# S5 states worked in place in PSUM: VectorE's products with one operand in a PSUM bank, and GpSimd's part between states and outputs dropped

## The chip, the cores and the metric

One core of a Trainium2 chip runs the kernel. The metric is the device time of the execution in microseconds, the median of several runs. PE is the matrix engine, DVE (VectorE), ACT (ScalarE) and POOL (GpSimd) work on SBUF; DVE and ACT also reach the PSUM banks into which PE writes, POOL does not in this kernel. SP issues DMA transfers. Each engine works through its own queue in order; semaphores hold an instruction until what it needs is done, and everything behind it on that engine waits too.

## The reference

A two-layer streaming encoder, one step: 512 tokens of a new stream and 32 of a running one, width 1024. Layer 0 mixes tokens with an S5 state-space layer and a GLU, layer 1 with retention; each layer then has attention to 256 memory tokens and a causal ConvFFN. The part that matters here:

```python
def s5_block(state, u, a_bar, b_bar, c):
    bu = jnp.einsum('gpc,blgc->blgp', b_bar, u.astype(jnp.complex64))
    bu = bu.at[:, 0].add(a_bar * state)
    a = jnp.broadcast_to(a_bar, bu.shape)
    _, xs = lax.associative_scan(_linear_combine, (a, bu), axis=1)
    y = jnp.real(jnp.einsum('gcp,blgp->blgc', c, xs))
    return xs[:, -1], y
...
    y = from_chunks(y).reshape(bsz, l, D_MODEL) + d.astype(F32) * hf
    g = jax.nn.gelu(y)
    out = g * jax.nn.sigmoid(g @ w_glu.astype(F32) + b_glu.astype(F32))
```

There are 64 groups of 16 channels, each with 64 complex states; `hf` is the RMS norm of x. The memory projections of both layers (`memory_kv`, 256 x 1024 by 1024 x 2048 each) depend on no token and can run at any time.

## The kernel before

Everything up to the GLU is `phase1`. Time is cut into blocks of 8 steps: 64 block positions for the prompt, 4 for the sample, and a few for initial states make POS = 70 positions. The recursion over 70 positions is a real scan, once the complex phase of each state is taken out: states are multiplied by a table of phases `pr`, `pi` (32 states a partition x 70), scanned with the real decay, and multiplied back. The channels are done in eight parts, e = 0 to 7 ("eighths": 8 groups each), and each eighth has six steps, which are functions inside `phase1`:

- **V** `powers(e)`: scales u by the RMS factor `ur` (POOL, L821) and forms powers of A times B: four VectorE products of 512 elements a partition (L829, L830) and two POOL additions (L831).
- **M** `matrices(e)`: PE transposes the powers (L843), ACT copies them out (L844); PE and ACT form the block's own matrix (L848, L850, L851), VectorE adds (Fg, L855) and SP spreads Fg by eight transfers (M<-Fg, L858).
- **S** `states(e)`: PE forms block inputs in two PSUM banks (L869, tile "bank"); VectorE multiplies by the phases (L884, L885, L887, L888: 280 elements), POOL subtracts and adds (L886, L889), and copies the initial state in (L890, L891).
- **Z** `scan(e)`: two VectorE scans (L902); four products by the phases, two on VectorE (L904, L906) and two on POOL (L905, L907); four sums L911/L912 of 64 partitions, which give S; ACT copies the end states into `stout` (L914, L915).
- **C** `carry(e)`: six VectorE instructions of 512 elements (L928, L930, L932) that form Y from the output coefficients `ca`.
- **O** `outputs(e)`: PE adds u by M (L943) and S by Y (L944) in a bank, ACT applies gelu (L945), PE transposes (L953), ACT copies out (L955, L956). The GLU's matmuls (L249) need all eight.

Between these steps `fill` puts pieces of the memory projections, which keep PE busy: layer 0 in plain fp32 (L528), layer 1 in two-part fp32 with three matmuls (L240, L241, L242). For layer 1 each weight tile is loaded (wr, L226), rounded on ACT (wh, L229), negated on ACT (wl, L230) and completed by an adding transfer that POOL issues (L235). Their results leave PSUM by VectorE (L550) or ACT (L565); L491 and L492 scale the memory tokens.

`PROLOGUE` and `ORDER` give the order in which the program writes these steps (at step e: S, C of e+1, V of e+3, Z of e+1, O of e, projections, M of e+2, projections). It is not the order of the queues: the framework plays the program through a timeline of its own (`schedule_with_timeline_sim=True`) and sorts each engine's instructions by it. The phase table is built by doubling in `phases` (L585 and L588 on POOL, L584, L586, L587, L589 on VectorE; L770 to L779 are the short chain that squares the phase). `ur` comes from a sum of squares on PE (L744), its reduction L746, and a short VectorE chain to L331. PSUM has eight banks in one ring (`bank()`), used in turn; SBUF has 28 slots "r" (`slot()`) and 8 slots "xl".

## Time and profile before

| what | us |
|---|---|
| median of 3 runs | 1877.81 (1876.53 to 1879.45) |
| the profiled execution | 1877.61 |
| its span | 1875.8 |
| PE busy in the span | 1814.0 |
| DVE busy | 1062.9 |
| ACT busy | 628.9 |
| POOL busy | 342.7 |
| first GLU matmul (L249) starts at | 233.61 |

Times in the profile are from the span's start. A group's row has its line, engine, operation, tiles (out<-in), shapes and count, then busy time and the mean of one in ns, then idle time of the engine ahead of it and what ended it. In the rows of the chain of waits and of the timeline the first number is the start, the second the length; the chain counts a piece up to where the next one begins, so that an instruction is shorter there by the overlap with its follower.

### The profile page before, as it was taken

To read this page: it belongs to the slowest core of one execution; us is meant where nothing else is said; L and a number is where in the kernel's file an instruction comes from. 1 tells how busy PE (TensorE), PEld (TensorE's weight loads), DVE (VectorE), ACT (ScalarE), POOL (GpSimd) and SP (SyncE) were. 2 spreads that over 40 slices of the span, in tenths; PEclk is the share of its full clock that TensorE was granted. 3 is DMA by queue.
4 is the path that set the end of the run, shared out by engine and by line. 5 is a ranking of instruction groups with operands and counts; after the bars stand their busy time and mean duration, and the time that the engine had idled before them with its cause. 6 is when DMAs were issued, how large, how long until landed. Compare 5 with 4: busy or idle time off the path is not lost.

```text
span 1875.8 us, 32777 instructions
## 1 busy us (share of the span) xinstructions
PE 1814.0 (97%) x13815; PEld 1727.9 (92%) x13815; DVE 1062.9 (57%) x1795; ACT 628.9 (34%) x933; POOL 342.7 (18%) x416
## 2 busy tenths in 40 slices
PE   8778899999999999999999999999999999999998
PEld 7467699999999999999899899998899999999997
DVE  8988875455535545555545645547654554453553
ACT  3244554343313323333123222223443332232333
POOL 4655410021202202220000100100101121120221
PEclk9978999999999999999999999999999999999999
DMA  6647743132222222222222222222312222222221
GB/s 227 201 122 176 193 159 103 56 107 82 90 83 86 82 99 89 82 91 85 82 88 85 71 88 74 91 79 90 124 68 68 79 91 90 84 81 96 90 72 68
DMA packets 68274, 186.41 MB, mean 99 GB/s; under 512 B 9184, under 2 KB 18784, under 8 KB 68128
## 3 DMA queue, kind: packets, MB, share of 16 engines
q1 hardware_dynamic: 65536, 175.79, 28.3%
q0 software_dynamic: 2304, 8.39, 2.5%
q8 instruction: 108, 1.77, 0.4%
q14 instruction: 38, 0.31, 0.1%
q10 hardware_dynamic: 288, 0.15, 0.0%
HBM read 171.16 MB, written 10.77 MB: 97 GB/s over the span
## 4 chain that ended last, share of the span: by engine, by line
PE 85%; DVE 8%; DMA 2%; issue 2%; ACT 2%; POOL 1%; SPq 0%; DVEq 0%; ACTq 0%; POOLq 0%
PE ps L249 75%; PE ps L240 2%; PE ps L241 2%; PE ps L242 2%; DMA M<-Fg 1%; DMA wr<-in_w_v 1%; PE ps L1341 1%; DVE r L902 1%; POOL u L821 1%; DVE r L830 1%; DVE wl L209 0%; PE ps L1330 0%; DVE r L930 0%; ACT wh L208 0%; PE ps L1303 0%
## 5 line engine op out<-in xcount | busy, mean ns | idle before, releaser
L249 PE MATMUL ps<-xh,wh 128*128 128x272 f32 x2432 | 505.2, 289 | 5.5 <-DVE x L372 3.7
L249 PE MATMUL ps<-xh,wl 128*128 128x272 f32 x2432 | 503.6, 288 | 0.0
L249 PE MATMUL ps<-xl,wh 128*128 128x272 f32 x2432 | 502.4, 288 | 0.0
L208 ACT CAST wh<-wr 128x1024 fp32r<-128x1024 f32 (+1 forms) x240 | 248.1, 1038 | 757.4 <-PE ps L249 640.0
L249 PE MATMUL ps<-r,wh 128*128 128x272 f32 x2688 | 448.1, 288 | 2.9 <-ACT r L956 1.6
L249 PEld LDWEIGHTS ps<-xh,wh 128*128 128x128 f32 x2432 | 381.8, 188 | 11.2 <-ACT r L314 3.8
L249 PEld LDWEIGHTS ps<-r,wh 128*128 128x128 f32 x2688 | 379.4, 188 | 6.3 <-ACT r L208 3.0
L249 PEld LDWEIGHTS ps<-xh,wl 128*128 128x128 f32 x2432 | 381.2, 188 | 2.3 <-issue 2.3
L249 PEld LDWEIGHTS ps<-xl,wh 128*128 128x128 f32 x2432 | 381.9, 188 | 0.3
L209 DVE TENSOR_TENSOR wl<-wr,wh 128x1024 fp32r<-128x1024 f32 (+1 forms) x240 | 296.1, 1237 | 94.9 <-ACT wh L208 86.7
L249 PE MATMUL ps<-r,wl 128*128 128x272 f32 x1344 | 277.9, 288 | 0.0
L249 PEld LDWEIGHTS ps<-r,wl 128*128 128x128 f32 x1344 | 210.7, 188 | 0.0
L372 DVE TENSOR_TENSOR x<-ps,x 128x544 f32<-128x544 f32 x96 | 69.3, 724 | 235.3 <-PE ps L249 234.9
L317 POOL TENSOR_TENSOR acc<-acc,r 128x544 f32<-128x544 f32 x36 | 59.2, 1645 | 452.4 <-ACT r L314 443.9
L1150 DVE TENSOR_TENSOR r<-ps,rr 128x544 f32<-128x544 f32 x44 | 31.9, 724 | 95.5 <-PE ps L249 95.5
L1140 DVE TENSOR_TENSOR r<-ps,rr 128x272 f32<-128x272 f32 x44 | 19.4, 442 | 116.9 <-PE ps L249 116.9
L1143 POOL COPY nco<-r 128x2 f32<-128x2 f32 x44 | 13.1, 297 | 373.5 <-DVE r L1141 373.5
L208 ACT CAST r<-r 128x544 fp32r<-128x544 f32 x84 | 52.5, 650 | 65.5 <-POOL r L1151 25.9
L1201 POOL TENSOR_TENSOR r<-r,r 128x544 f32<-128x544 f32 x8 | 10.8, 1354 | 339.7 <-ACT wh L208 325.7
L1151 POOL TENSOR_TENSOR r<-r,r 128x32 f32<-128x32 f32 x44 | 35.0, 795 | 206.3 <-ACT wh L208 191.1
L1148 DVE SCALAR_TENSOR_TENSOR r<-r,conv,r 128x546 f32<-128x546 f32 x88 | 69.1, 785 | 3.5 <-ACT r L1146 2.0
L209 DVE TENSOR_TENSOR r<-r,r 128x544 fp32r<-128x544 f32 x84 | 59.3, 728 | 10.6 <-ACT r L208 10.4
(347 smaller groups left out, 2102.0 us busy)
## 6 DMA issues: line engine op xcount, KB each, us to landing
wr<-in_w_r SPq DMA_DIRECT2D x48, 512.0 KB, 3.3
wr<-in_w_a SPq DMA_DIRECT2D x44, 512.0 KB, 3.2
wr<-in_w_g SPq DMA_DIRECT2D x44, 512.0 KB, 3.3
wr<-in_w_d SPq DMA_DIRECT2D x32, 448.0 KB, 3.3
wr<-in_w_k SPq DMA_DIRECT2D x16, 512.0 KB, 4.1
wr<-in_w_v SPq DMA_DIRECT2D x16, 512.0 KB, 4.0
wr<-in_w_q SPq DMA_DIRECT2D x16, 512.0 KB, 3.8
wr<-in_w_o SPq DMA_DIRECT2D x16, 512.0 KB, 3.3
```

The lines of the kernel that those rows point to most:

```text
L208: self.nc.scalar.copy(hi, src)
L209: (self.nc.gpsimd if pool else self.nc.vector).tensor_tensor(out=lo, in0=src, in1=hi.bitcast(F32), op=OP.subtract)
L240: mm(out, lhsT=a[0], rhs=b[0], start=start, stop=False)
L241: mm(out, lhsT=a[0], rhs=b[1], start=False, stop=False)
L242: mm(out, lhsT=a[1], rhs=b[0], start=False, stop=stop)
L249: mm(ps[:, h, :TH], lhsT=ws[wi], rhs=x[xi][:, h * TH:(h + 1) * TH], start=start and n == 0, stop=stop and n == 2)
L317: add.tensor_tensor(out=self.acc, in0=self.acc, in1=sq, op=OP.add)
L372: self.nc.vector.tensor_tensor(out=self.halves(x), in0=src, in1=self.halves(x), op=OP.add)
L1140: V.tensor_tensor(out=ext[:, 2:2 + TH], in0=pa[:, 0, :TH], in1=r[:, :TH], op=OP.mult)
L1148: V.scalar_tensor_tensor(out=cv, in0=ext[:, t:t + W], scalar=cw[:, t, f:f + 1], in1=cv, op0=OP.mult, op1=OP.add)
L1150: V.tensor_tensor(out=self.halves(gr), in0=pg[:, :, :TH], in1=self.halves(r), op=OP.mult)
L1151: PL.tensor_tensor(out=gr[:, TP:], in0=gr[:, TP:], in1=cv[:, TP + 2:W], op=OP.mult)
```

## The change

The state banks stay in use from PE's products until the sums: S multiplies into SBUF and in place in the bank, the subtraction and the addition are VectorE's and write the bank, the scan works in place on the bank, and so does one of each pair of products behind it. So each VectorE instruction there has one operand in PSUM and at most one in SBUF. POOL's L886, L889, L905 and L907 go to VectorE; its copies L890 and L891 go to ACT (L899, L898). The coefficients that C and V read are copied by ACT into free columns of the state banks (columns 280 to 408: `ca`, L880; 408 to 472: the b coefficients of eighth e+2, L884, for e = 1 to 5; those of eighths 0 to 2 lie in a bank of their own, L816). C's second product goes into a bank of the ring instead of an SBUF slot, and the load of `ca` is issued in S instead of C. New line numbers: L821 is L826, L829/L830/L831 are L834/L835/L836, L844 is L849, L855 is L860, L869 is L876, the products of S are L893/L894, the subtraction and addition L897/L896, the scan L915, its products L916/L917, the sums L921/L922, `stout` L924/L925, C is L938/L940/L942, gelu L955, the outputs' matmuls L953/L954.

```diff
+        b3 = self.bank()[:, :384].rearrange("p (n e i c) -> p n e i c", n=2, e=3, i=4)
+        for n in range(2):
+            A.copy(b3[:, n], bb[n][:, :12].rearrange("p (e i) c -> p e i c", e=3))
+        bbe = {e: [b3[:, n, e] for n in range(2)] for e in range(3)}
...
-            bs = [a[:, p0:p0 + 4].unsqueeze(2).to_broadcast(sh) for a in bb]
+            bs = [a.unsqueeze(2).to_broadcast(sh) for a in bbe.pop(e, [b[:, p0:p0 + 4] for b in bb])]
...
         def states(e):
+            ca = load("ca", [P, 2, 8, C], io["ca"][e].rearrange("p (r n c) -> p r n c", r=2, n=8), 2)
+            banks = [self.bank() for _ in range(2)]
+            d["v"] = v = [b[:, :280].rearrange("p (n q) -> p n q", n=4) for b in banks]
...
+            d["ca"] = [b[:, 280:408].rearrange("p (n c) -> p n c", c=C) for b in banks]
+            for n in range(2):
+                A.copy(d["ca"][n], ca[:, n])
+            if e and e + 2 < KT:
+                bbe[e + 2] = [b[:, 408:472].rearrange("p (n c) -> p n c", c=C) for b in banks]
+                for n in range(2):
+                    A.copy(bbe[e + 2][n], bb[n][:, p0 + 8:p0 + 12])
...
-            V.tensor_tensor(out=w[0], in0=vps[0], in1=phs[0], op=OP.mult)
-            V.tensor_tensor(out=x1[0], in0=vps[1], in1=phs[1], op=OP.mult)
-            PL.tensor_tensor(out=w[0], in0=w[0], in1=x1[0], op=OP.subtract)
-            V.tensor_tensor(out=w[1], in0=vps[1], in1=phs[0], op=OP.mult)
-            V.tensor_tensor(out=x1[1], in0=vps[0], in1=phs[1], op=OP.mult)
-            PL.tensor_tensor(out=w[1], in0=w[1], in1=x1[1], op=OP.add)
-            PL.tensor_copy(out=w[0][:, :, 65], in_=s0[:, p0:p0 + 4])
-            PL.tensor_copy(out=w[1][:, :, 65], in_=s0n[:, p0:p0 + 4])
+            x = d["x"] = pair()
+            for n in range(2):
+                V.tensor_tensor(out=x[n], in0=v[n], in1=phs[0], op=OP.mult)
+                V.tensor_tensor(out=v[n], in0=v[n], in1=phs[1], op=OP.mult)
+            V.tensor_tensor(out=v[1], in0=x[0], in1=v[1], op=OP.subtract)
+            V.tensor_tensor(out=v[0], in0=x[1], in1=v[0], op=OP.add)
+            A.copy(v[1][:, :, 65], s0[:, p0:p0 + 4])
+            A.copy(v[0][:, :, 65], s0n[:, p0:p0 + 4])
...
         def scan(e):
+            z = d["v"][::-1]
+            x = pair()
             for n in range(2):
-                V.tensor_tensor_scan(out=z[n].rearrange("p n q -> p (n q)"), data0=d0.rearrange("p n q -> p (n q)"),
-                                     data1=w[n].rearrange("p n q -> p (n q)"), initial=0.0, op0=OP.mult, op1=OP.add)
-            V.tensor_tensor(out=x1[0], in0=z[0], in1=phs[0], op=OP.mult)
-            PL.tensor_tensor(out=x1[1], in0=z[1], in1=phs[1], op=OP.mult)
-            V.tensor_tensor(out=x2[0], in0=z[1], in1=phs[0], op=OP.mult)
-            PL.tensor_tensor(out=x2[1], in0=z[0], in1=phs[1], op=OP.mult)
+                zn = z[n].rearrange("p n q -> p (n q)")
+                V.tensor_tensor_scan(out=zn, data0=d0, data1=zn, initial=0.0, op0=OP.mult, op1=OP.add)
+                V.tensor_tensor(out=x[n], in0=z[n], in1=phs[0], op=OP.mult)
+                V.tensor_tensor(out=z[n], in0=z[n], in1=phs[1], op=OP.mult)
...
         def carry(e):
-            ca = load("ca", [P, 2, 8, C], io["ca"][e].rearrange("p (r n c) -> p r n c", r=2, n=8), 2)
+            ca = d["ca"]
...
-                y, yt = xl(512), self.slot(512)
+                y, yt = xl(512), self.bank()
```

The change also alters the sorted order of the queues. Three places follow, each with the queue before and then after; r is an SBUF slot, bank a PSUM bank, and a number behind a name tells one tile from another.

POOL before, from the phase table's products (ph) to the scaling of u:

```order
L585 TENSOR_TENSOR r_608<-ph_506 128x480
L588 TENSOR_TENSOR r_609<-ph_506 128x480
L585 TENSOR_TENSOR r_616<-ph_506 128x512
L588 TENSOR_TENSOR r_617<-ph_506 128x512
L831 TENSOR_TENSOR r_673<-r_673,r_675 128x512
L831 TENSOR_TENSOR r_674<-r_674,r_676 128x512
L821 TENSOR_TENSOR u_158<-u_158,ur_451 128x560
L821 TENSOR_TENSOR u_159<-u_159,ur_451 128x560
```

POOL now, in the same part of the program:

```order
L826 TENSOR_TENSOR u_164<-u_164,ur_451 128x560
L826 TENSOR_TENSOR u_165<-u_165,ur_451 128x560
L585 TENSOR_TENSOR r_551<-ph_506 128x32
L588 TENSOR_TENSOR r_552<-ph_506 128x32
L836 TENSOR_TENSOR r_516<-r_516,r_518 128x512
L836 TENSOR_TENSOR r_517<-r_517,r_519 128x512
L807 COPY ph_506<-ph_506 128x32x5
L585 TENSOR_TENSOR r_566<-ph_506 128x96
L588 TENSOR_TENSOR r_567<-ph_506 128x96
```

The eight scalings of u stood behind all products of the phase table; now all of these, from the first doubling (128x32) on, stand behind the scalings.

VectorE before, from the first carry to the scan of eighth 0:

```order
L928 TENSOR_TENSOR xl_717<-ca_715,Pr_351 128x512
L928 TENSOR_TENSOR xl_722<-ca_715,Pr_351 128x512
L884 TENSOR_TENSOR r_703<-bank_683,ph_506 128x280
L888 TENSOR_TENSOR r_704<-bank_683,ph_506 128x280
L855 TENSOR_TENSOR Fg_659<-bank_647,Fg_659 128x128
L885 TENSOR_TENSOR r_704<-bank_692,ph_506 128x280
L887 TENSOR_TENSOR r_703<-bank_692,ph_506 128x280
L930 TENSOR_TENSOR r_718<-ca_715,ait_381 128x512
L930 TENSOR_TENSOR r_723<-ca_715,ait_381 128x512
L928 TENSOR_TENSOR xl_874<-ca_872,Pr_351 128x512
L928 TENSOR_TENSOR xl_879<-ca_872,Pr_351 128x512
L932 TENSOR_TENSOR xl_717<-xl_717,r_718 128x512
```

VectorE now, from the first products of eighth 0 on:

```order
L893 TENSOR_TENSOR r_710<-bank_688,ph_506 128x280
L893 TENSOR_TENSOR r_710<-bank_689,ph_506 128x280
L894 TENSOR_TENSOR bank_688<-bank_688,ph_506 128x280
L894 TENSOR_TENSOR bank_689<-bank_689,ph_506 128x280
L897 TENSOR_TENSOR bank_688<-r_710,bank_688 128x280
L896 TENSOR_TENSOR bank_689<-r_710,bank_689 128x280
L938 TENSOR_TENSOR xl_719<-bank_688,Pr_351 128x512
L938 TENSOR_TENSOR xl_724<-bank_688,Pr_351 128x512
L940 TENSOR_TENSOR bank_720<-bank_689,ait_381 128x512
L940 TENSOR_TENSOR bank_725<-bank_689,ait_381 128x512
L915 SCALAR_TENSOR_TENSOR bank_688<-d_150_708,bank_688 128x280
L942 TENSOR_TENSOR xl_719<-xl_719,bank_720 128x512
```

The carry of eighth 0 stood ahead of its products and partly beside POOL's work; now its products come first, the subtraction and addition follow on VectorE, and the carry behind them reads and writes banks.

ACT before, from the copy of eighth 2's end states on (wh and wl are rounded weights of the projections):

```order
L914 COPY stout_498<-r_1100 128x8
L915 COPY stout_498<-r_1100 128x8
L229 CAST wh_1218<-wr_1216 128x1024
L844 COPY xl_1178<-bank_1180 128x512
L844 COPY xl_1179<-bank_1186 128x512
L230 ACTIVATE wl_1219<-wh_1218 128x1024
L850 COPY ft_1201<-bank_1192 128x128
L229 CAST wh_1253<-wr_1251 128x1024
L230 ACTIVATE wl_1254<-wh_1253 128x1024
L229 CAST wh_1394<-wr_1392 128x1024
L230 ACTIVATE wl_1395<-wh_1394 128x1024
```

ACT now, from the end states of eighth 2 on, with the copies into the banks of eighth 3 (bank_1294, bank_1295):

```order
L924 COPY stout_498<-r_1107 128x8
L925 COPY stout_498<-r_1107 128x8
L849 COPY xl_1185<-bank_1187 128x512
L849 COPY xl_1186<-bank_1193 128x512
L230 ACTIVATE wl_1226<-wh_1225 128x1024
L855 COPY ft_1208<-bank_1199 128x128
L229 CAST wh_1260<-wr_1258 128x1024
L230 ACTIVATE wl_1261<-wh_1260 128x1024
L229 CAST wh_1403<-wr_1401 128x1024
L880 COPY bank_1294<-ca_1292 128x128
L230 ACTIVATE wl_1404<-wh_1403 128x1024
L884 COPY bank_1294<-bbr_402 128x64
```

The copies of the coefficients stand behind the copy of the end states and behind the conversions of the projections' weights, mixed with them.

More of the change, by code (lines that the diff above doesn't have):

```diff
@@ L881, in states, with pair @@
                              in1=rho8[:, p0:p0 + 4].unsqueeze(2).to_broadcast(pos3), op=OP.mult)
[L882 to L892 removed]
+            x = d["x"] = pair()
[6 more added lines that the diff above has]
+            A.copy(v[0][:, :, 65], s0n[:, p0:p0 + 4])
+        def pair():
+            t = self.slot(SLOT)
+            return [t[:, n * 280:(n + 1) * 280].rearrange("p (n q) -> p n q", n=4) for n in range(2)]
         def scan(e):
@@ L910, in scan @@
                 r = slice(64 * g2, 64 * g2 + 64)
[L911 to L912 removed]
+                V.tensor_tensor(out=SS[0:64, :, g2], in0=x[0][r], in1=z[1][r], op=OP.add)
+                V.tensor_tensor(out=SS[64:128, :, g2], in0=x[1][r], in1=z[0][r], op=OP.subtract)
             S = d["S"] = SS.rearrange("p n g q -> p (n g) q")
```

21 lines of the change are left out of this document (4 added, 17 removed).

## The prediction

> **What bounds the kernel now.** I read the windows first, to find the stage that the change touches and who is busy in it, then PE's waits there, then VectorE's groups by shape, and at last the chain of waits through the stage. The windows' columns: from:to, length, then busy time (and instructions) of PE, PEld, DVE, ACT and POOL, the granted clock, the DMA share, GB/s.
>
> ```profile
> 93.00:234.00 141.00, 111.17 (x951) 97.41 (x952) 119.54 (x178) 64.85 (x128) 71.14 (x78) 0.88 0.66 164
> 180.00:220.00 40.00, 36.54 (x328) 30.71 (x328) 33.84 (x51) 20.44 (x36) 20.66 (x26) 0.99 0.88 211
> 234.00:1875.80 1641.80, 1623.78 (x12485) 1574.75 (x12483) 863.11 (x1404) 537.22 (x762) 219.44 (x276) 1.00 0.26 87
> ```
>
> Behind 234 us PE works 1623.78 of 1641.80 us at full clock. The built order of PE is the same there before and after: its last 12,271 matmuls stand in the same sequence. So the whole change is what it does to the time at which the GLU's first matmul (L249) starts; that shift passes through one to one. Ahead of it, from 93 to 234, PE idles 141.00 - 111.17 = 29.8 us and VectorE is busy 119.5 of 141.
>
> ```profile
> PE bank L944 <- DVE r L911: 8.5, 2, 7.8
> PE bank L944 <- DVE r L912: 6.3, 1, 6.3
> PE bank L241 <- DVE r L492: 5.2, 1, 5.2
> ```
>
> PE's longest waits in this stage are for VectorE: for an eighth's sums L911/L912 (the outputs' second matmul needs them), and for L492. The groups of VectorE, and the same lines in the chain of waits (start, length; the lengths run from start to start):
>
> ```profile
> L930 DVE TENSOR_TENSOR r<-ca,ait 128x512 f32<-128x512 f32 x16 | 20.1, 1294 | 0.0
> L932 DVE TENSOR_TENSOR xl<-xl,r 128x512 f32<-128x512 f32 x16 | 16.4, 1058 | 0.0
> L928 DVE TENSOR_TENSOR xl<-ca,Pr 128x512 f32<-128x512 f32 x15 | 14.0, 971 | 0.1
> L902 DVE TENSOR_TENSOR_SCAN r<-d,r 128x280 f32<-128x280 f32 x16 | 13.7, 890 | 1.9 <-POOL r L890 1.8
> L884 DVE TENSOR_TENSOR r<-bank,ph 128x280 f32<-128x280 f32 x8 | 3.6, 445 | 0.6 <-PE bank L869 0.5
> L855 DVE TENSOR_TENSOR Fg<-bank,Fg 128x128 f32<-128x128 f32 x8 | 2.3, 282 | 2.0 <-PE bank L851 2.0
> ```
>
> ```profile
> 92.97 0.45 DVE r L911
> ...
> 110.43 1.58 DVE r L492 x4
> ...
> 118.70 0.35 DVE r L887
> ...
> 120.86 1.29 DVE r L930 x2
> 122.15 0.60 DVE r L829
> ...
> 171.13 1.28 DVE r L902 x2
> ...
> 220.58 1.20 DVE xl L932 x2
> ...
> 226.43 0.46 DVE r L911
> ...
> 233.61 2.40 PE ps L249 x17
> ```
>
> With POOL out of the way a 512-wide product or sum takes 0.60 us and a scan 0.64; the means of the same lines are 0.97 to 1.29 and 0.89. The products that read PSUM (L884) stay at 0.445 busy, 0.35 from start to start. From the last sum of eighth 0 (92.97+0.45 = 93.42) to that of eighth 7 (226.89) the recursion takes 133.5 us; the GLU follows 6.7 us later, at 233.61.
>
> **What leaves and what is added.** POOL loses six instructions an eighth:
>
> ```profile
> L889 POOL TENSOR_TENSOR r<-r,r 128x280 f32<-128x280 f32 x8 | 8.8, 1100 | 0.0
> L907 POOL TENSOR_TENSOR r<-r,ph 128x280 f32<-128x280 f32 x8 | 8.6, 1081 | 6.8 <-DVE r L902 6.8
> L905 POOL TENSOR_TENSOR r<-r,ph 128x280 f32<-128x280 f32 x8 | 7.6, 945 | 0.7 <-DVE r L902 0.7
> L886 POOL TENSOR_TENSOR r<-r,r 128x280 f32<-128x280 f32 x8 | 7.2, 900 | 16.9 <-DVE r L885 16.9
> L890 POOL COPY r<-s 128x4 f32<-128x4 f32 x8 | 5.5, 685 | 0.0
> L891 POOL COPY r<-s0n 128x4 f32<-128x4 f32 x8 | 5.3, 663 | 0.0
> ```
>
> That is 43.0 us of POOL. VectorE takes over four of them, 0.36 us each: 8 x 4 x 0.36 = 11.5 us more. In return its stretched lines fall to the undisturbed times: L930 16 x 0.69 = 11.1, L932 16 x 0.46 = 7.3, L928 15 x 0.37 = 5.6, scans 16 x 0.25 = 4.0, together 28.0, and L830, L904, L906, L912 and the hand-overs to POOL on top.
>
> One eighth of VectorE's work in the new order, undisturbed: four products and the subtraction and addition 6 x 0.36 = 2.2; L938, L940, L942 and the four powers L834/L835 of the eighth after next 10 x 0.60 = 6.0; two scans 1.3, four products 1.4, four sums 4 x 0.43 = 1.7. That is 12.6; without powers (eighths 6 and 7) 10.2. About 0.4 is added, because L938 now waits for ACT's copy of the initial state (L899) into the same bank: 13.0 and 10.6.
>
> VectorE has no instruction in this trace that writes PSUM, and ten an eighth will (80 in all, in place or L940). From 128 to 280 elements a PSUM read grows from 0.282 to 0.445, so its fixed part is about 0.15. The ends I allow are that part saved or paid twice: 80 x 0.15 = 12 us either way. I take zero, the nearest row being L884, whose other end is in SBUF.
>
> [...]
>
> **What moves: the front.** POOL's scaling of u (L821, now L826) stands ahead of the phase table's products L585/L588 in the new order; before, it stood behind them.
>
> ```profile
> 45.65 7.71 PE L744 MATMUL bank<-r,block 128*128 128x280 f32 x32
> 68.84 0.44 DVE L746 TENSOR_REDUCE ssum<-bank 128x70 f32<-128x280 f32 x1
> 72.33 12.48 POOL L821 TENSOR_TENSOR u<-u,ur 128x560 f32<-128x560 f32 x8 [5.42 <-ACT ft L850]
> 74.73 0.45 DVE L884 TENSOR_TENSOR r<-bank,ph 128x280 f32<-128x280 f32 x1 [0.26 <-PE bank L869]
> 97.63 1.27 POOL L831 TENSOR_TENSOR r<-r,r 128x512 f32<-128x512 f32 x1 [0.69 <-DVE r L830]
> L585 POOL TENSOR_TENSOR r<-ph 128x480 f32<-128x480 f32 (+4 forms) x6 | 6.1, 1013 | 10.0 <-DVE ph L779 10.0
> L588 POOL TENSOR_TENSOR r<-ph 128x480 f32<-128x480 f32 (+4 forms) x6 | 6.0, 997 | 0.0
> ```
>
> The norm's sum (L746) can run when L744 is done, at 53.4, and no longer at 68.84; its chain took until 72.3 (3.4 us), so ur is there at 56.7. Eight scalings at 1.27 x 560/512 = 1.39 end at 67.9. Only then do the phase products run: 12.1 us, two additions L836 at 1.27 ahead of most of them, 0.7 of copies, and some 3 us in which POOL waits for VectorE's half of a round: 86.2, and the last sums 86.5. Eighth 0's first product moves from 74.73 to 86.5, 11.8 us later. Before, it then stood until POOL had finished with u; after, it runs its 13.0 us through: sums at 99.5, 6.1 us late. The cover of this is gone: PE has finished the layer-0 projections by then and idles.
>
> **What is added as a wait: ACT's copies.** From eighth 2 on, the first product L893 waits for the coefficient copies L880 and L884 into its bank, and they stand in ACT's queue behind the stout copies L924/L925 (these wait for the eighth before's sums) and behind weight conversions.
>
> ```profile
> L229 ACT CAST wh<-wr 128x1024 fp32r<-128x1024 f32 x15 | 15.8, 1050 | 21.6 <-PE bank L241 13.1 <-DMA M<-Fg 3.6 <-PE bank L242 3.3
> L230 ACT ACTIVATE wl<-wh 128x1024 fp32r<-128x1024 f32 x15 | 15.9, 1062 | 0.3
> L844 ACT COPY xl<-bank 128x512 f32<-128x512 f32 x14 | 7.7, 595 | 1.9 <-PE bank L843 1.9
> L914 ACT COPY stout<-r 128x8 f32<-128x8 f32 x8 | 1.6, 204 | 43.5 <-DVE r L911 39.2 <-DVE r L912 4.3
> ```
>
> A small copy into PSUM is not in the trace; between 0.20 (L914) and 0.60 (L844) I take 0.25. Eighth 3 in the order: L924, L925, two L849, L230, L855, L229, L230, L229, L880, L230, L884. That is 5 conversions at 1.06 (5.3), 1.2, and 1.1 of small ones: 7.6 us from the sums of eighth 2 to the first product. Counted in the same way: eighth 2 has 3.0, eighth 4 6.8, eighth 5 8.6, eighth 6 2.2, eighth 7 5.7. Eighth 1 has none (its bank was filled early), but eight L492 and L860 stand ahead, 4.0 us. Sums to sums: 17.0, 16.0, 20.6, 19.8, 21.6, 12.8, 16.3 = 124.1 us, against 133.5.
>
> **The smaller moves.** The carry's second product now lies in a PSUM bank, so the transposes L848 wait for L942 in the ring of banks; at eighth 2 PE is held to 112 us, where it stood for L492 before (the 5.2 us row). O(0)'s gelu stands behind L899/L898 of eighth 1 on ACT: PE loses some 6 us there, out of its 29.8 idle. The load of ca moves ahead by a stage on SP and waits for ACT's copies of two eighths earlier; it is needed a step later, so zero. Late in the stage the outputs O(4) and O(6) stand behind projection matmuls that wait for ACT (L230) and then for POOL's weight transfer:
>
> ```profile
> wl<-in_w_v POOLq DMA_DIRECT2D x8, 512.0 KB, 6.4
> ```
>
> I find PE there within about 1.5 us of the sums, on either side: zero, with 1.5 us for the range.
>
> **The sum.** 6.1 late at the front, 133.5 - 124.1 = 9.4 gained over seven eighths: 3.3 us. POOL's additions L836, and L492 and L550 on VectorE, which I took at their old durations, lose their share of the disturbance too. I put 0.8 us on that, a little over one 512-wide line's excess (L930: 1.294 - 0.60): 4.1 us. The profiled execution took 1877.61 us (span 1875.8), within 0.2 of the median 1877.81, so 1873.5.
>
> **Rivals.** *VectorE was the bound and ACT's waits hide.* The 28.0 less 11.5 is 16.5 us, with the hand-overs (a POOL subtraction and its two copies, about 2 us of waiting an eighth) some 20; less the front's 6.1, about 14: 1863.5. For it: VectorE's 119.5 of 141. Against it: the conversions stand in ACT's order in front of the copies. Chance 0.17.
>
> *ACT's queue becomes the bound: slower.* The conversion L229 ahead of the copies must itself wait for a weight tile, which SP issues behind the eight transfers M<-Fg. In the quoted row ACT already waits for these (3.6). If at eighths 3, 4, 5 and 7 the tile lands 4 us late, that is 16 us, less the 4.1: 1889; from 1 us each on, the gain is gone, and from 2 us each the kernel is slower by 0.2%. For it: ACT's wait rows; against it: PE holds those conversions back longer (13.1) than transfers do. Chance 0.24.
>
> *Swallowed before the GLU.* From 180 to 220 PE is busy 36.54 of 40 at clock 0.99 and DMA 0.88. If weight tiles set the pace there, what is gained earlier is lost again and 1 to 2 us remain either way: 1877. Chance 0.18.
>
> *Writing PSUM is dear.* Each of the 80 instructions that write a bank pays its fixed part twice, the upper end above: 12 us on VectorE's path, and 1885.5. For it only that no row shows such a write; against it, that reading a bank costs nothing extra. Chance 0.04.
>
> **How the numbers follow.** About 0.2% (3.75 us) is what a measurement of this kernel can tell from no change. My forecast has 0.37; its own range is 1869 to 1877, so 0.29 of it is faster by more than 0.2% and 0.08 within. Faster 0.29 + 0.17 = 0.46; same 0.08 + 0.18 = 0.26; slower 0.24 + 0.04 = 0.28. The range goes from 1862 (the forecast with the lower PSUM end, 1861.5, and nearly the first rival's 1863.5) to 1886 (the upper PSUM end, 1885.5), which leaves out the far part of the second rival, about 0.12, and the tail of the first, 0.06.
>
> **What would show it.** Right: the first L893 near 86 us and the first sums near 100; L938, L940 and L942 at 0.60 and scans at 0.64 throughout; L893 waiting for ACT L884 by 2 to 9 us in eighths 2 to 5 and 7; the first L249 near 229.5. Wrong: L893 before 80 us (the front did not slip), scans or products on PSUM well off 0.64 and 0.36, ACT's L229 waiting for transfers ahead of L880, or L249's start moved by over 8 us.

## The result, and the profile after

The changed kernel takes 1889.14 us (median of 4 runs, 1888.11 to 1889.96) against 1878.63 (4 runs) for the kernel before on the same chip: a ratio of 1.0055, with the 95% interval from 1.0038 to 1.0073. It is 10.5 us slower. The forecast was 1873.5, with a range of 1862 to 1886. The profiled execution took 1889.96, its span 1888.1.

The windows first: the stretch of the prediction, and then the first 20 us of the GLU, of the kernel after (the first two rows) and of the kernel before (the last):

```profile
93.00:234.00 141.00, 109.49 (x939) 94.20 (x935) 104.56 (x217) 67.56 (x155) 33.06 (x38) 0.87 0.61 152
243.04:263.04 20.00, 20.00 (x149) 20.00 (x150) 11.07 (x16) 10.71 (x16) 0.00 (x0) 0.93 0.46 161
```

```profile
233.61:253.61 20.00, 20.00 (x160) 20.00 (x160) 11.58 (x16) 11.50 (x17) 0.00 (x0) 1.00 0.52 176
```

VectorE has become lighter in the stretch (104.56 us of 141, before 119.54) and POOL has lost more than half (33.06, before 71.14). PE still does less (109.49, before 111.17). All three are idle for more of the stretch. The GLU's first matmul starts at 243.04 instead of 233.61, and its first 20 us hold 149 matmuls at a granted clock of 0.93 instead of 160 at 1.00.

VectorE's groups after, in the stretch from 73 to 245 us:

```profile
L915 DVE TENSOR_TENSOR_SCAN bank<-d,bank 128x280 f32<-128x280 f32 x16 | 11.2, 729 | 0.0
L940 DVE TENSOR_TENSOR bank<-bank,ait 128x512 f32<-128x512 f32 x16 | 10.3, 689 | 0.0
L938 DVE TENSOR_TENSOR xl<-bank,Pr 128x512 f32<-128x512 f32 x16 | 10.3, 682 | 7.4 <-ACT bank L899 7.4
L942 DVE TENSOR_TENSOR xl<-xl,bank 128x512 f32<-128x512 f32 x16 | 10.2, 676 | 0.0
...
L894 DVE TENSOR_TENSOR bank<-bank,ph 128x280 f32<-128x280 f32 x16 | 7.0, 446 | 0.0
...
L893 DVE TENSOR_TENSOR r<-bank,ph 128x280 f32<-128x280 f32 x16 | 7.0, 441 | 9.2 <-ACT bank L884 8.8 <-ACT bank L880 0.4
...
L209 DVE TENSOR_TENSOR wl<-wr,wh 128x1024 fp32r<-128x1024 f32 x3 | 3.7, 1226 | 6.5 <-ACT wh L208 6.5
```

The long instructions do what was forecast: L938, L940, L942 and the scan fall from 0.89 to 1.29 us to 0.68 to 0.73. Writing a bank in place (L894, 446 ns) costs no more than writing SBUF (L893, 441). What is new stands in the last column: VectorE waits for ACT. The waits that grew, in the stretch from 73 to 250 (total, times, longest):

```profile
ACT wh L229 <- PE bank L242: 8.7, 2, 7.9
...
DVE xl L938 <- ACT bank L899: 7.4, 2, 7.2
...
PE bank L848 <- POOL r L836: 7.2, 2, 6.7
PE bank L241 <- DMA wl<-in_w_v: 6.6, 2, 5.1
```

L848 belongs to the front, whose powers' addition on POOL comes late. The longest waits of the other three are one event, in eighth 5. The timeline there (start, length, in brackets the wait ahead of it):

```profile
178.71 0.87 POOL L235 DMA_DIRECT2D wl<-in_w_v  x1 [2.70 <-ACT ft L855]
...
186.04 0.79 PE L241 MATMUL bank<-wl,r 128*128 128x512 f32 x1 [5.08 <-DMA wl<-in_w_v]
...
191.14 1.05 ACT L229 CAST wh<-wr 128x1024 fp32r<-128x1024 f32 x1 [7.89 <-PE bank L242]
...
192.09 0.16 ACT L899 COPY bank<-s0n 128x4 f32<-128x4 f32 x1
...
192.28 1.29 DVE L938 TENSOR_TENSOR xl<-bank,Pr 128x512 f32<-128x512 f32 x2 [7.21 <-ACT bank L899]
...
194.38 0.38 PE L953 MATMUL bank<-M,u 128*69 128x128 f32 x2
```

From the top: POOL issues a weight transfer at 178.71. PE has 26 projection matmuls in its queue, and behind them eighth 4's outputs (L953). The projection comes to its turn before the tile is in and waits 5.08 us for it. ACT's next conversion L229 waits for these matmuls to free the weight tile. The small copy L899 stands behind L229. VectorE's carry L938 waits for L899. So one weight tile that is not there yet stops three engines at once, and the outputs of eighth 4, whose sums were ready at 175.2, start at 194.38.

Eighth 7 has a smaller form of it:

```profile
221.81 1.23 DVE L209 TENSOR_TENSOR wl<-wr,wh 128x1024 fp32r<-128x1024 f32 x1 [5.84 <-ACT wh L208]
...
226.43 1.23 DVE L209 TENSOR_TENSOR wl<-wr,wh 128x1024 fp32r<-128x1024 f32 x1 [0.39 <-ACT wh L208]
...
227.29 0.50 PE L241 MATMUL bank<-wl,r 128*128 128x512 f32 x1 [1.52 <-DMA wl<-in_w_v]
...
231.59 1.23 DVE L209 TENSOR_TENSOR wl<-wr,wh 128x1024 fp32r<-128x1024 f32 x1 [0.31 <-ACT wh L208]
...
236.80 0.44 PE L954 MATMUL bank<-xl,r 128*69 128x128 f32 x2 [1.58 <-DVE r L922]
```

Subtractions for the GLU's weights (L209) stand in VectorE's queue ahead of and between the products, carry and scans of the last eighth, on which the whole GLU waits. In the kernel before, one of them stood there too, ahead of the products and with a shorter wait; the others stood behind the sums:

```profile
215.49 1.22 DVE L209 TENSOR_TENSOR wl<-wr,wh 128x1024 fp32r<-128x1024 f32 x1 [3.17 <-ACT wh L208]
```

Read off the timelines, the ends of each eighth's sums (0 to 7), and the start of L249:

| kernel | 0 | 1 | 2 | 3 | 4 | 5 | 6 | 7 | L249 |
|---|---|---|---|---|---|---|---|---|---|
| before | 93.9 | 120.8 | 133.6 | 156.2 | 176.9 | 197.3 | 211.0 | 226.9 | 233.6 |
| after | 105.0 | 121.2 | 137.3 | 156.8 | 175.2 | 202.9 | 216.0 | 237.2 | 243.0 |

The front is 11.1 us late and by eighth 1 nothing is left of that. At eighth 4 the changed kernel is 1.7 us ahead. Eighth 5 then costs 27.7 us where 20.4 stood before, eighth 7 21.2 instead of 15.9: 7.3 and 5.3 us. The lead of 1.7, these two and 0.6 won in eighth 6 make the 10.3 us at the last sums. Behind them 0.9 is won up to L249, and 2.9 more is lost behind it: 12.3 in these two executions.

### The profile page after: what moved, and what is told of

Read it like the earlier page. It is cut to its first block, busy times and chain, and to the rows that moved or that the text cites. A ratio compares the mean times of both kernels' runs of the same rounds, so it can differ in the third digit from the quotient of the medians.

```text
span 1888.1 us, 32839 instructions
## 1 busy us (share of the span) xinstructions
PE 1821.8 (96%) x13815; PEld 1732.8 (92%) x13815; DVE 1036.9 (55%) x1827; ACT 636.5 (34%) x977; POOL 293.1 (16%) x368
## 4 chain that ended last, share of the span: by engine, by line
PE 84%; DVE 2%; ACT 1%; issue 1%; DMA 0%; ACTq 0%; DVEq 0%
PE ps L249 75%; PE ps L240 2%; PE ps L241 2%; PE ps L242 2%; PE ps L1351 1%; DVE wl L209 1%; PE ps L1340 0%; PE ps L1313 0%; PE ps L1073 0%; ACT wh L208 0%; PE ps L1287 0%; DMA wl<-in_w_v 0%; PE bank L1087 0%; DVE xl L308 0%; PE ps L345 0%
## 5 line engine op out<-in xcount | busy, mean ns | idle before, releaser
L249 PE MATMUL ps<-xh,wh 128*128 128x272 f32 x2432 | 507.5, 290 | 5.4 <-DVE x L372 3.6
L249 PE MATMUL ps<-xl,wh 128*128 128x272 f32 x2432 | 503.6, 288 | 0.0
L249 PE MATMUL ps<-xh,wl 128*128 128x272 f32 x2432 | 502.3, 288 | 0.0
L249 PE MATMUL ps<-r,wh 128*128 128x272 f32 x2688 | 449.0, 289 | 3.0 <-ACT r L966 1.6
L249 PEld LDWEIGHTS ps<-xh,wh 128*128 128x128 f32 x2432 | 380.6, 188 | 11.2 <-ACT r L314 3.8
L249 PEld LDWEIGHTS ps<-r,wh 128*128 128x128 f32 x2688 | 379.9, 189 | 6.4 <-ACT r L208 3.0
L249 PEld LDWEIGHTS ps<-xh,wl 128*128 128x128 f32 x2432 | 382.0, 188 | 2.3 <-issue 2.3
L249 PEld LDWEIGHTS ps<-xl,wh 128*128 128x128 f32 x2432 | 383.0, 189 | 0.3
L209 DVE TENSOR_TENSOR wl<-wr,wh 128x1024 fp32r<-128x1024 f32 (+1 forms) x240 | 296.8, 1239 | 98.0 <-ACT wh L208 89.2
L249 PE MATMUL ps<-r,wl 128*128 128x272 f32 x1344 | 278.1, 288 | 0.0
L249 PEld LDWEIGHTS ps<-r,wl 128*128 128x128 f32 x1344 | 211.1, 189 | 0.0
L209 DVE TENSOR_TENSOR r<-r,r 128x544 fp32r<-128x544 f32 x84 | 59.3, 728 | 12.8 <-ACT r L208 12.6
```

What stands on the lines that cost most here:

```text
L209: (self.nc.gpsimd if pool else self.nc.vector).tensor_tensor(out=lo, in0=src, in1=hi.bitcast(F32), op=OP.subtract)
L249: mm(ps[:, h, :TH], lhsT=ws[wi], rhs=x[xi][:, h * TH:(h + 1) * TH], start=start and n == 0, stop=stop and n == 2)
```

## Experiments

Each was timed in three rounds beside the kernel before on the same chip, whose median there lay between 1877.5 and 1879.2. The ratios are to it. A difference in us between two changed kernels is one of medians, often from different chips, so two kernels whose intervals overlap are hardly told apart by it. The name behind "Measured" is that of the run. "Sums" are the ends of an eighth's sums in the trace.

### The order of ACT, VectorE and POOL

`behind(a, b)` below puts instruction a after b in one engine's queue and adds no wait; the framework sorts the rest anew around it, so small moves elsewhere ride along. First, the weight conversions behind the initial-state copies of the S written before them:

```diff
+        self.behind(self.nc.scalar.copy(hi, raw), self.s_last)        # L229
...
+            self.s_last = (A.copy(v[1][:, :, 65], ...), A.copy(v[0][:, :, 65], ...))
```

> The changed kernel with one order rule on ACT and no other edit: every weight conversion of the projections that is written after an eighth's states is queued behind that eighth's two initial-state copies. Theory Q (queues): the loss is made where a short instruction of the recursion stands behind a long one of the projections. Here it is eighth 5, whose carry waited 7.2 us for ACT's copy, which stood behind a conversion held by PE. Q expects that wait gone, eighth 5's sums about 6 us earlier and the time 4 to 7 us below the changed kernel, 1882 to 1885. Theory F (front): the 11.6 us by which eighth 0's sums slipped is the loss and everything behind only passes it on; F expects less than 1 us of change, 1888 to 1890. Theory T (transfers): the adding weight transfers set the pace from 175 us on; T expects 1888 to 1892, the conversions being later.

Measured (act_order): 1887.66 (ratio 1.0048, 1.0033 to 1.0063). Eighth 5's step falls by 8.4 to 19.3 us, as theory Q said, but the time only by 1.5, which the intervals don't tell from nothing. Eighths 6 and 7 take 18.9 and 22.7, 7.3 more together, and from the last sums to L249 it is 2.7 more. PE still waits 3.8 us for a weight transfer (the wait ahead of L247, the L241 of above): ACT's copy was moved out of the way of that wait, and the wait stayed. Why eighths 6 and 7 grew was not followed up.

Second, the subtractions L209 of weights behind the last sums written before them, for the GLU's weights those of eighth 7:

```diff
+        if not pool:
+            self.behind(sub, self.z_last)                             # L209
...
+                self.z_last = (V.tensor_tensor(out=SS[0:64, :, g2], ...), V.tensor_tensor(out=SS[64:128, :, g2], ...))
```

> The changed kernel with one order rule on VectorE: the low parts of the GLU's first weight tiles (L209) are queued behind the sums of eighth 7 instead of ahead of and among its work. Q expects the 3.7 us of L209 and most of its 5.8 us wait out of eighth 7's way, eighth 7's sums 4 us earlier and 3 to 4 us off the time, 1885 to 1886. F and T expect less than 1 us, 1888 to 1890.

Measured (dve_order): 1885.58 (1.0033, 1.0019 to 1.0048): 3.6 us less, the size that theory Q named. The intervals overlap, though all of these runs (up to 1886.07) lie below all of the changed kernel's (from 1888.11). Eighth 7's sums come 2.5 us earlier instead of 4, and L249 2.2 us earlier. The rest goes with the GLU's first 20 us, which hold 159 matmuls at a granted clock of 1.00 here against 149 at 0.93, so the order alone is worth some 2 us.

Third, the scalings of u for eighths 1 to 7 behind the phase table again:

```diff
+            self.behind(PL.tensor_tensor(out=u, in0=u, in1=ur..., op=OP.mult), self.ph_last)    # L826
...
+        self.cm_last = (e2.tensor_tensor(out=t[1], in0=ai, in1=br, op=OP.mult),)           # L588
```

> The changed kernel with one order rule on POOL: the scalings of u of eighths 1 to 7 are queued behind the phase table's products, as they were before the change; that of eighth 0 stays ahead. Eighth 0's first product should move from 91.9 to about 82 us. F expects all of it at the end: 8 to 10 us less, 1879 to 1881. Q expects it to be passed on too as long as no queue holds it, and part of it to be lost at eighth 5, where ACT's copy waits for PE: 3 to 7 us less, 1882 to 1886. T expects under 2 us, 1887 to 1889.

Measured (front_order): 1888.61 (1.0056, 1.004 to 1.0072). That is the range of theory T, but the edit did not do what it was for: the first product comes at 89.5 instead of 91.9, not near 82, so the time speaks for none of the three. The timeline shows why:

```profile
71.59 11.38 DVE L593 TENSOR_TENSOR ph<-ph 128x512 f32<-128x512 f32 x1
...
72.57 1.27 POOL L594 TENSOR_TENSOR r<-ph 128x512 f32<-128x512 f32 x1
...
73.64 8.77 POOL L833 TENSOR_TENSOR u<-u,ur 128x560 f32<-128x560 f32 x7
```

L593 is a product of the phase table's last doubling on VectorE (L587 in the changed kernel). With both operands in SBUF it stands for 11.38 us beside POOL's run of seven scalings, and the products behind it stand too; the same instruction takes 0.68 us in the kernel after. So POOL's run was moved, and moved into the way of the last doubling.

### Taking the change apart

If POOL's part is dropped and nothing is put into PSUM:

```diff
-            PL.tensor_tensor(out=w[0], in0=w[0], in1=x1[0], op=OP.subtract)
+            V.tensor_tensor(out=w[0], in0=w[0], in1=x1[0], op=OP.subtract)
...
-            PL.tensor_copy(out=w[0][:, :, 65], in_=s0[:, p0:p0 + 4])
+            A.copy(w[0][:, :, 65], s0[:, p0:p0 + 4])
```

(and so L889, L891, L905, L907 of the kernel before.)

> The kernel before with only POOL's part dropped: the subtraction, the addition and two of the four products behind the scan go to VectorE, the initial-state copies to ACT; every operand stays in SBUF, no coefficients are copied into banks, and the carry keeps its SBUF slot. POOL's queue at the front keeps its order. If it is POOL's part that stretched VectorE's instructions, these fall towards 0.60 and 0.36 us here as well and the time falls by 4 to 8 us below the kernel before, 1871 to 1875. If it is the second SBUF operand as such, they stay near 1 us beside POOL's remaining work and, with 11.5 us of VectorE work more, the time is 0 to 6 us above the kernel before.

Measured (sbuf_products): 1867.47 (1863.1 to 1870.75; ratio 0.994, 0.9919 to 0.9962). It is 10.6 us faster than the kernel before and 21.7 faster than the changed kernel. Its VectorE groups from 60 to 226 us:

```profile
L928 DVE TENSOR_TENSOR xl<-ca,Pr 128x512 f32<-128x512 f32 x16 | 13.1, 854 | 0.1
L930 DVE TENSOR_TENSOR r<-ca,ait 128x512 f32<-128x512 f32 x16 | 12.2, 805 | 0.0
L902 DVE TENSOR_TENSOR_SCAN r<-d,r 128x280 f32<-128x280 f32 x16 | 11.2, 738 | 0.0
L932 DVE TENSOR_TENSOR xl<-xl,r 128x512 f32<-128x512 f32 x16 | 10.5, 692 | 0.0
L830 DVE TENSOR_TENSOR r<-PIn,bbr 128x512 f32<-128x512 f32 x7 | 10.2, 1456 | 0.0
...
L905 DVE TENSOR_TENSOR r<-r,ph 128x280 f32<-128x280 f32 x8 | 3.5, 437 | 0.0
```

The scan and the sum L932 are as short as with PSUM operands. L930 has won four fifths of what it can win (1294 to 805, with 689 in PSUM), L928 two fifths (971 to 854, with 682). L830, which still runs beside POOL's L831, keeps most of its length (1638 before, in the same window). So in the carry and the scan most of VectorE's relief comes from POOL doing less. L905, with both operands in SBUF, is needed further down.

Now the two halves of the PSUM edit, each by itself. The state half: products, scan and sums in place in the state banks, all coefficients read from SBUF.

```diff
-            bs = [... for a in bbe.pop(e, [b[:, p0:p0 + 4] for b in bb])]
+            bs = [... for a in [b[:, p0:p0 + 4] for b in bb]]
...
-            d["ca"] = [b[:, 280:408].rearrange("p (n c) -> p n c", c=C) for b in banks]
-                A.copy(d["ca"][n], ca[:, n])
...
-                y, yt = xl(512), self.bank()
+                y, yt = xl(512), self.slot(512)
```

> Only the state half of the PSUM edit: states are multiplied, scanned and summed in place in their banks, the initial states are copied into these banks, and VectorE does POOL's part; the carry and the powers read their coefficients from SBUF, and no bank copies of coefficients are made. Theory C (the coefficient copies cost the time: they move POOL's scaling of u ahead of the phase table and put ACT's queue ahead of the first product): first product near 75, sums of eighth 0 at or below 97, 1866 to 1872. Rival S (working in place costs it: the scan's second half of the bank is tied to ACT's copy of the initial state, and the banks are held from the states to the sums): 1880 to 1888, with the first GLU matmul behind 236.

Measured (states_in_bank): 1863.29 (0.992, 0.9903 to 0.9938). Sums of eighth 0 at 92.8, of eighth 7 at 209.4. Working in place costs nothing that shows, and may give: it is 4.2 us below the version with SBUF products, with intervals that overlap.

The coefficient half: powers and carry read ACT's copies in banks, the carry's second product lies in a bank, the states are worked in SBUF.

```diff
+        b3 = self.bank()[:, :384].rearrange("p (n e i c) -> p n e i c", n=2, e=3, i=4)
...
+                A.copy(d["ca"][n], ca[:, n])
...
+                    A.copy(bbe[e + 2][n], bb[n][:, p0 + 8:p0 + 12])
...
-                y, yt = xl(512), self.slot(512)
+                y, yt = xl(512), self.bank()
```

(against the version with SBUF products)

> Only the coefficient half of the PSUM edit: the powers and the carry read ACT's copies in PSUM banks and the carry's second product lies in a bank, while the states are multiplied, scanned and summed in SBUF (all on VectorE, as in the version with SBUF products). Theory C: first product behind 85, sums of eighth 0 behind 98, waits for L884-type copies on ACT, 1880 to 1890. Rival S: 1866 to 1873, first GLU matmul ahead of 228. Its built order has POOL's eight scalings of u ahead of the phase table, as the changed kernel has; so if only the front costs, 1873 to 1880.

Measured (coef_in_bank): 1885.31 (1.0042, 1.0028 to 1.0057); first product at 89.9, sums of eighth 0 at 104.3. The loss is in this half: 17.8 us against the version with SBUF products.

The changed kernel without the powers' copies (L816, L884):

```diff
-        b3 = self.bank()[:, :384].rearrange("p (n e i c) -> p n e i c", n=2, e=3, i=4)
-            A.copy(b3[:, n], bb[n][:, :12].rearrange("p (e i) c -> p e i c", e=3))
...
-                    A.copy(bbe[e + 2][n], bb[n][:, p0 + 8:p0 + 12])
```

> The changed kernel, with the powers' coefficients read from SBUF: the early bank with three eighths' coefficients and the copies for eighths 3 to 7 are gone, the carry's copies and the carry's bank stay. Its built order has POOL's phase table ahead of the scalings of u again. If the front slip is most of the loss: first product 74 to 77, sums of eighth 0 at or below 98, 1878 to 1884. Rival (what the front loses is made up again by the weights' queue, and eighths 5 and 7 cost the time): first product early, but the first GLU matmul still behind 239 and 1886 to 1890.

Measured (powers_sbuf): 1891.84 (1.0075, 1.0058 to 1.0092). The front is whole again: first product at 75.2, sums of eighth 0 at 89.8, 15 us earlier than in the changed kernel, yet L249 starts at 246.97. An early front, which several expectations made most of the loss, is worth nothing here: by eighth 3 the sums (156.1) are where the changed kernel has them (156.8). VectorE waits 14.0 us in this stage for ACT's copy L876 and PE 27.3 us for ACT's gelu.

What is left between 1863 and 1892 are two edits: the carry's copies of `ca` (ACT, L880) and the carry's second product in a bank.

```diff
-                y, yt = xl(512), self.slot(512)
+                y, yt = xl(512), self.bank()
```

> The version with states worked in place in their banks (1863.3), with one thing more of the change: the carry's second product lies in a PSUM bank instead of an SBUF slot, so two more tenants an eighth pass through the ring of eight banks. Theory B (the ring is the cost: projections, matrices and outputs wait for banks that the states and the carry hold): 1878 to 1890, with waits of PE for the carry's addition and for ACT's gelu. Rival A (the coefficient copies on ACT are the cost): 1861 to 1867.

Measured (carry_bank), with states in their banks and this edit alone: 1863.06 (0.9919, 0.9903 to 0.9936). Two more tenants an eighth in the ring of banks cost nothing that can be told.

```diff
+            d["ca"] = [b[:, 280:408].rearrange("p (n c) -> p n c", c=C) for b in banks]
+            for n in range(2):
+                A.copy(d["ca"][n], ca[:, n])
```

> The version with states worked in place (1863.3), with the other thing: ACT copies the carry's coefficients into the state banks ahead of the first product, and the carry reads them there; its second product stays in an SBUF slot. Theory A: the first product waits for the second of these copies (7 us and more in several eighths) and 1878 to 1890. Rival B: 1863 to 1867.

Measured (carry_coef), with the carry's copies alone (and the load of `ca` issued in S, as in the change): 1872.08 (0.9967, 0.9955 to 0.9979), 8.8 us more than without them. Alone -0.2 and +8.8, together (1891.84) +28.5: the two edits are not additive.

### Why the copies cost

Three readings were possible: the tie between the first product and ACT's copy, ACT's queue, and the banks being held longer.

```diff
-            d["ca"] = [...]; A.copy(d["ca"][n], ca[:, n])      # ahead of the products
...
             A.copy(v[0][:, :, 65], s0n[:, p0:p0 + 4])
+            d["ca"] = [...]; A.copy(d["ca"][n], ca[:, n])      # behind the initial states
```

> As the one with the carry's coefficients copied into the state banks, but the two copies are written behind the initial-state copies, that is behind the products and the in-place additions, so that no product waits for them; the carry still reads the copies. Theory A (the place in ACT's queue ahead of the first product is what costs): 1862 to 1870. If the copies cost wherever they stand (ACT busy, or the carry now waits for them): within 4 us of the version with early copies.

Measured (coef_late): 1879.91 (1.0009, 0.9999 to 1.0018). With the copies behind the products no product waits for them, and it is 7.8 us slower still. The tie as such was the wrong answer, and the time lies in neither expected range.

> The version with the carry's coefficients copied into the state banks (1872.1), with ACT's two copies going into an SBUF slot instead: ACT's instructions stay, but no product waits for them and the bank is free after the sums. Theory Q in the strict form (the tie between the first product and the copy is the cost): 1862 to 1867. If ACT's work as such costs: 1870 to 1875. Rival H: 1862 to 1867 as well, so this run speaks for or against ACT's work alone.

```diff
-            d["ca"] = [b[:, 280:408].rearrange("p (n c) -> p n c", c=C) for b in banks]
+            cs = self.slot(256)
+            d["ca"] = [cs[:, n * 128:(n + 1) * 128].rearrange("p (n c) -> p n c", c=C) for n in range(2)]
```

Measured (coef_slot): 1866.87 (0.9937, 0.9921 to 0.9953). The same 16 copies by ACT into SBUF, with the earlier load of `ca`, cost 3.6 us over none. The intervals overlap, so ACT's work is a small part at most. The other 5.2 us go with the copies lying in the state banks; the tie and the longer hold of the bank are both in them.

In the changed kernel, all copies by VectorE (L816 and L884 in the same way):

```diff
-                A.copy(d["ca"][n], ca[:, n])
+                V.tensor_copy(out=d["ca"][n], in_=ca[:, n])
```

> The changed kernel with all its bank copies of coefficients (L816, L880, L884) made by VectorE instead of ACT; banks, their tenants and all operands stay as in the changed kernel. Theory Q (VectorE waits for copies that stand in ACT's queue behind conversions and behind waits for VectorE itself): no product waits for ACT any more, and 1865 to 1876, though VectorE has some 30 copies more. Rival H (a bank with coefficients in it is held until the carry and the powers of two eighths later have read them, and the ring of eight banks runs dry): 1882 to 1892.

Measured (copies_on_vector): 1890.87 (1.0065, 1.005 to 1.008). All 28 copies are taken from ACT and nothing is won, though VectorE's own time for them may hide a few us. The rows of waits from 73 to 245 us show the same event without them:

```profile
PE bank L241 <- DMA wl<-in_w_v: 7.1, 2, 5.8
...
DVE bank L940 <- ACT bank L898: 7.6, 1, 7.6
```

So the copies' place in ACT's queue is not what stops eighth 5; what VectorE waits for there is the initial-state copy behind a conversion.

In the changed kernel:

```diff
-                y, yt = xl(512), self.bank()
+                y, yt = xl(512), self.slot(512)
```

> The changed kernel with the carry's second product in an SBUF slot instead of a bank; all copies stay on ACT. If copies and the carry's bank cost more together than apart (H, or ACT's queue and the ring interlocked): 1870 to 1880. If the copies alone make the loss (Q): 1884 to 1890.

Measured (carry_slot): 1884.41 (1.0026, 1.0013 to 1.0038): 4.7 us less than the changed kernel, at the edge of the second expectation, with intervals that touch. Here the carry's bank costs something, and the copies the most.

### PE's order

The built queues of all these kernels show one thing that goes with the time. In the four that have both the copied coefficients and the carry's second product in banks (the changed kernel, coef_in_bank, powers_sbuf and copies_on_vector, 1885 to 1892 us), 26 to 36 projection matmuls of layer 1 stand between eighth 5's state products and eighth 4's outputs, and the last 15 or 17 ahead of eighth 6's outputs. The three order experiments above (act_order, dve_order, front_order) have kept this. In all other kernels, the one before among them, eighth 4's outputs stand first. Two of these, carry_slot and coef_late, take 1884 and 1880 all the same, so this order can't be the whole loss. The timeline by which the framework sorts does that; no line of the program says it. To see whether it is the cause, it was changed by itself, in the changed kernel:

```diff
+        self.behind(mm(out, lhsT=a[0], rhs=b[0], ...), self.o_last)     # L240
...
+                    self.o_last = (nc.tensor.matmul(o, lhsT=S[:, g, 0:69], ...),)   # L954
```

> The changed kernel with one edge of order on PE: the projections' matmuls that are written behind an eighth's output matmuls stand behind them in the built order too. So eighths 4 and 6 have the outputs ahead of the projections, as the kernel before and all faster variants have. All instructions, banks and copies are the changed kernel's. Theory O (PE's built order is the larger part of the loss): eighth 5's wait for ACT goes or shrinks to under 3 us, sums of eighth 7 by 230, 1876 to 1883. Rival H (banks): 1886 to 1891.

Measured (pe_order): 1884.24 (1.0031, 1.0018 to 1.0043), 4.9 us faster than the changed kernel. That is just above the expected 1883, and the intervals overlap at their edges, but all of these runs (up to 1885.96) lie below all of the changed kernel's (from 1888.11). The place in eighth 5, in the timeline of this run (L905 is the L899 of above, L944 is L938, L247 is L241, and POOL's L241 is the L235 of above):

```profile
178.63 0.87 POOL L241 DMA_DIRECT2D wl<-in_w_v  x1 [2.60 <-ACT ft L861]
...
184.68 0.17 ACT L905 COPY bank<-s0n 128x4 f32<-128x4 f32 x1 [1.51 <-DVE bank L903]
...
184.91 1.28 DVE L944 TENSOR_TENSOR xl<-bank,Pr 128x512 f32<-128x512 f32 x2
...
186.81 0.50 PE L247 MATMUL bank<-wl,r 128*128 128x512 f32 x1 [2.47 <-DMA wl<-in_w_v]
...
189.67 1.05 ACT L235 CAST wh<-wr 128x1024 fp32r<-128x1024 f32 x1 [3.42 <-PE bank L248]
```

The carry starts at 184.91 instead of 192.28, and its wait of 7.21 us is gone. POOL issues the transfer at 178.63, as in the changed kernel (178.71), and PE's projection starts no earlier, at 186.81. So the tile was not late; the matmul stood too early. PE still waits 2.47 us for it, but the outputs are done and VectorE's carry does not hang on it. Eighth 5's step is 20.4 us, as in the kernel before.

With VectorE's edge added:

```diff
+        if not pool:
+            self.behind(sub, self.z_last)                             # L209
```

> As the last, and VectorE's subtractions of the GLU's weights (L209) stand behind eighth 7's sums. Theory O: the two gains add, 1872 to 1880, that is no slower than the kernel before. Rival H: the gain of the VectorE order alone, 1883 to 1888.

Measured (pe_dve_order): 1881.44 (1.0011, 1.0002 to 1.0021): sums of eighth 7 at 228.3 and L249 at 235.03, 8 us earlier than in the changed kernel. The time lies just outside the first expectation: the second edge adds 2.8 us. By the medians the two edges of order take back 7.7 of the 10.5 us. In the same runs the kernel is 2.2 us behind the one before, which is just above nothing.

### Attempts at the best version

The powers' additions (L831) on VectorE as well, in the version with SBUF products, in the one with states in their banks, and in the one that has the carry's product in a bank too:

```diff
-                PL.tensor_tensor(out=vb[n], in0=vb[n], in1=vt[n], op=OP.add)
+                V.tensor_tensor(out=vb[n], in0=vb[n], in1=vt[n], op=OP.add)
```

> The version with SBUF products, with the additions of the powers (L831) moved from POOL to VectorE too. If POOL's disturbance of VectorE's two-SBUF-operand instructions is what counts: L830 falls from 1.46 to 0.6-0.7, 1860 to 1866. Rival: VectorE is the bound and its 14 additions of about 0.6 us (8.4 us) outweigh that, or the weight transfers set the end: 1867 to 1873.

> The version with states worked in place (1863.3), with the powers' additions on VectorE instead of POOL. If POOL's contention still stretches VectorE there: 1858 to 1862. If VectorE's own length sets the pace by now, or the weight transfers do: 1862 to 1867.

> The version with states in their banks and the carry's second product in a bank (1863.1), with the powers' additions on VectorE, so that POOL keeps the scalings of u, the phase table, the decays, Fg and the weight transfers. Attempt at the best version: 1856 to 1862; if the GLU's weights set the end by now: 1861 to 1865.

Measured (sbuf_all, states_all, carry_bank_all): 1861.62 (0.9918, 0.9903 to 0.9933), 1861.77 (0.9912, 0.9893 to 0.9931) and 1860.5 (0.9904, 0.9887 to 0.9921). These cannot be told from each other, and hardly from the versions without the edit (1867.5, 1863.3 and 1863.1): the gain is 5.9, 1.5 and 2.6 us, with intervals that overlap. In sbuf_all L830 falls to 0.69 us, as expected. All three beat the kernel before by 0.8 to 1.0%. In the last, L249 starts at 215.30.

## Why the prediction was wrong, step by step

**VectorE's relief: right.** L938, L940, L942 and scans are at 0.60 and 0.64 from start to start, as forecast. The rows show who is held: L593 of front_order, with two SBUF inputs, took 11.38 us beside POOL's scalings, and two L942 of the changed kernel, with one each, took 1.27 us together beside POOL's L836 (from 197.07 and 197.11 on). What I missed is that taking POOL's work away gives most of that relief without any PSUM operand (1867.5).

**PSUM writes at zero: right.** L894, which writes a bank, takes 446 ns, and L893, which writes SBUF, 441. L905 of sbuf_products, as wide and out of SBUF alone, takes 437. These rows differ by less than 0.01 us. And states_in_bank is not slower than the version with SBUF products (1863.29 against 1867.47).

**The front: mis-sized by 5.5 us.** I had the first product at 86.5 and the first sums at 99.5; they came at 91.9 and 105.0. POOL scaled from 57.94 to 67.83, against 56.7 to 67.9 as worked out; that the end fits is partly luck, since the late start and the shorter scalings cancel. Then VectorE's half of the table was held by POOL's (one L587 took 5.30 us). I had priced POOL's half and some 3 us of its waits for VectorE, and not this stretch of VectorE's half. Against the kernel before, the late front left little: eighth 1's sums ended at 121.2, before at 120.8. What the front costs by itself was not shown. front_order did not bring it back, and powers_sbuf, with its sums of eighth 0 15 us earlier, has the longest time of all.

**The seven steps: five right, two wrong.** Forecast 17.0, 16.0, 20.6, 19.8, 21.6, 12.8, 16.3; measured 16.2, 16.1, 19.5, 18.4, 27.7, 13.1, 21.2. Five are within 1.4 us and 2.9 better in sum; eighth 5 is 6.1 and eighth 7 is 4.9 worse.

**The step that failed** is the one under the smaller moves: "I find PE there within about 1.5 us of the sums, on either side: zero". I had seen O(4) and O(6) behind the projections, and that these wait for ACT and POOL's transfer, and I costed PE's lateness alone. The wait does not stay on PE: the missing tile holds PE's matmuls, these hold ACT's next conversion, that holds the initial-state copy behind it, and that holds VectorE's carry for 7.21 us. The edge of order in pe_order prices it at 4.9 us. Eighth 7's part was a term that the prediction did not have at all: the GLU's subtractions L209 among VectorE's work, which wait 6.5 us for ACT. Without them there the step falls from 21.2 to 18.6 (dve_order), so 2.3 us against my 16.3 stay unexplained; both edges together take back 7.7 us. The second rival had ACT's queue and a time of 1889, and its number came out by luck: it had the wait at the first product L893 in four eighths (8.8 us in four pieces in the trace) where the one that decided was at L938, and it named SP's loads landing late at L229 as the origin, for which L229 never waits behind 100 us in the trace, instead of PE's order.

**The shift passes through behind L249: not quite.** From L249 to the end the changed kernel takes 1645.06 us, the one before 1642.19. 11 matmuls fewer in the first 20 us are 1.4 us of these 2.9, by the lower clock (0.93 against 1.00); the rest I can't place. Twelve of the twenty kernels start the GLU at a clock of 0.91 to 0.93, states_in_bank and carry_bank_all among them, and powers_sbuf, the slowest, starts it at 1.00: it is not a mark of the loss.

**The sum, by its own terms:** 5.5 us for the front, -2.9 and +11.0 for the steps, 0.8 of relief that was put on top and didn't show, -0.9 up to L249, +2.9 behind it: 16.4, the distance from 1873.5 to 1889.96.

**What stays open.** With both orders undone, 2.2 us against the kernel before and 18 against states_in_bank remain; so the coefficient half costs more than these two orders. The copies' work (3.6 us on ACT, not clear of noise), their lying in the state banks (5.2) and the non-additive rest with the carry's bank were measured, and how the last comes about was not settled; nor is the 7.8 us by which coef_late, with no tie to the products, is slower than carry_coef. Why the framework's timeline puts the projections first when both edits are there was not tried either: its order goes with the two edits together, in four kernels of four.

## What to carry to other kernels

Where a scheduler sorts the queues, compare their orders after every edit, and look above all at what stands behind a matmul that waits for a transfer: follow that wait from engine to engine until it ends, since its price is not the idle time of the engine where it starts. Ahead of moving operands into PSUM to get out of GpSimd's way, try taking GpSimd's work away: here that was 10.6 us of gain for a few lines. PSUM operands added some 4 more at most, not clear of noise, and only where no coefficients had to be copied into the banks. Take a change of several parts apart before judging it: of its two PSUM halves one was worth about -4 us, not clear of noise, and the other +18.

## What the hardware showed unexpectedly

- A VectorE instruction with two SBUF operands was held not for one POOL instruction but for a whole run of them: 11.38 us beside seven scalings of 8.77 us in all, and 5.30 in the kernel after beside four products of the phase table. Undisturbed these instructions took 0.68 and 0.65.
- In-place VectorE work on a PSUM bank (product, sum or scan, 280 elements) takes about what it takes in SBUF undisturbed: the product 446 ns against 437 (L905 of sbuf_products), the scan 729 against 738 (its L902), and the sum 445, for which no undisturbed SBUF row of the same shape was read.
- The GLU's first 20 us ran at a granted clock of 0.91 to 0.93 in twelve of the twenty kernels, with 147 to 149 matmuls, and at 1.00 in the other eight, the kernel before among them, with 159 or 160. Fast and slow kernels are in both groups.
